# A branch for short expert tiles: gate and up on 32 columns of the array

## The chip, the cores and the metric

The kernel runs on one core of a Trainium2 chip. The metric is the device time of one execution, in microseconds (us). Five engines work beside each other, each with its own stream of instructions: TensorE (PE; its weight loads are PEld), VectorE (DVE), ScalarE (ACT), GpSimd (POOL) and SyncE (SP), which here only starts weight transfers. Each engine branches for itself. A name with a q (PEq, DVEq) is the engine's sequencer.

## The reference, cut to what matters

One decoder layer over 512 tokens of 1024 channels: a mixer (a state-space branch and an attention branch), then a mixture of 16 experts. The change lies in the experts. Each token is sent to two of them:

```
for e in range(16):
    hid = silu(t @ w_gate[e]) * (t @ w_up[e])      # 1024 -> 512, twice
    out = out + gates[:, e:e+1] * (hid @ w_down[e])  # 512 -> 1024
```

with `gates` zero for all but the token's two experts. The kernel computes an expert only for its own tokens, in float32.

## The kernel before, in words

**Stages.** The mixer takes the first 560 us or so, then come routing and, from 577 to 898 us, the experts; a last normalisation ends the kernel. Nothing before or behind the expert stage changes, but for one more small buffer (`sgs`, line 1123) that is cleared early.

**Tiles.** An expert's tokens are cut into tiles of H = 64. A gathered tile `xg` has 128 rows: 64 tokens times two halves of 512 channels. `x_columns` (line 1178) transposes it into `xT`. `body(e, t)` (line 1313) does tile t of expert e in this order on TensorE: `up` (line 1286), then the down product of the tile before (`down`, line 1301; so the silu and the multiplication of this tile have time), `x_columns` of tiles to come, `hidden_columns` (line 1296, transposes of the hidden values) and, for t = 0, the token lists of expert e + 2 (`tile_tokens`, line 1174), which turn ranks into the indices that GpSimd gathers by.

**Gate and up.** `up` runs over 8 parts k of the 1024 channels. For each, the 64 tokens' columns are the stationary operand and 512 columns of the gate weights move through the left half of the array (64 of its columns), 512 of the up weights through the right half. The results stand in one PSUM bank: gate in partitions 0 to 63, up in 64 to 127. `hidden` (line 1292) takes silu of the lower half and multiplies it by the upper.

**Branches.** Tile 0 always runs. Tiles 1 and 2 stand in `tc.If` blocks on the expert's token count (lines 1355 and 1357); tile 2's block lies in that of tile 1. A fourth and later tiles run in ten nested blocks behind the loop (line 1421), which these inputs don't need. What stands in such a block is scheduled as a unit; code outside can be moved ahead of it. That is done today: `up` of the next expert's tile 0 is code outside any block, and a few of its products are issued ahead of line 1355's branch.

**Weights.** An expert has six pieces of 1 MB, loaded by SP into 18 buffers in turn, so three experts ahead; `drop` frees pieces once an expert's products are done, and SP's next transfers start then.

**Order.** `in_order` keeps the written order of TensorE, VectorE and ScalarE instructions within one `with`, not from one `with` to the next.

Of the kernel before, what the change touches and what calls it, by code (L numbers as in the profile page):

```python
# [13 lines left out]
AF = mybir.ActivationFunctionType  # L14
ALU = mybir.AluOpType
AX = mybir.AxisListType

P = 128
# [3 lines left out]
KT = D // P  # L22
# [6 lines left out]
UNIT = 512  # L29
EVAC = 400  # L30
DUE = 8, 4, 4
H = P // 2
INL = 3
MAXO = 10

# [72 lines left out]
def hybrid_layer(ctx: ExitStack, tc: tile.TileContext, A, out):  # L108
    nc = tc.nc
# [127 lines left out]
    class Stream:  # L237
# [7 lines left out]
        def add(self, units, loads, parts):  # L245
            for n, part in enumerate(parts):
                self.parts.append((len(self.raws), n == len(parts) - 1) + part)
            self.raws.append((units, loads))
# [96 lines left out]
    class Experts:  # L345
# [18 lines left out]
        def up(self, e, k):  # L364

            assert self.nload >= 6 * e + 4
            return [self.piece(6 * e + 2 * (k // 4) + n)[:, k % 4 * FF:(k % 4 + 1) * FF] for n in range(2)]

        def down(self, e, k):
            assert self.nload >= 6 * e + 6  # L370
            return [self.piece(6 * e + 4 + k // 2)[:, k % 2 * D + n * 512:k % 2 * D + (n + 1) * 512]
                    for n in range(2)]
# [5 lines left out]
    ew = Experts([(wg_all[e], wu_all[e], wd_all[e]) for e in range(NE)], [])  # L378
# [25 lines left out]
    for j in range(4):  # L404
# [14 lines left out]
        for t, sc_ in enumerate((1, 0)):  # L419
            o = 8 * sc_ + 2 * j  # L420
# [142 lines left out]
    for g in range(4):  # L563
# [17 lines left out]
        for c in range(NT):  # L581
            nc.tensor.matmul(pt[:, c * P:(c + 1) * P], Bc.ap[:, c * P:(c + 1) * P], Cc.ap[:, c * P:(c + 1) * P],
                             start=True, stop=True)
# [14 lines left out]
        for c2 in range(2):  # L598
            pt = tr.get()
            for c in (2 * c2, 2 * c2 + 1):  # L600
                for t in range(2):
                    o = (c % 2) * 256 + t * P
# [19 lines left out]
        for c in (1, 2):  # L622
# [4 lines left out]
                                    op=ALU.add)  # L627
# [71 lines left out]
    for j in range(4):  # L699
# [14 lines left out]
        for hh in range(2):  # L714
            m = FM.alloc(1)
            nc.vector.tensor_tensor(m.v(NT, P), fr[hh].v(NT, P), negm[:, None, :].to_broadcast([P, NT, P]),
                                    op=ALU.subtract)
# [4 lines left out]
        for i in range(NT):  # L722
            w = (i + 1) * P
# [36 lines left out]
        o = FM.alloc(1)  # L760
# [82 lines left out]
    for j in range(8):  # L843
        for y in (ys[j], ya[j]):
            pt = proj(hT, KT)
            t = FM.alloc(1)
# [18 lines left out]
    def rtile(nm, shape, dt=F32):  # L865
        if dt is I32:
            return cp.tile(shape, dt, name=f"rt_{nm}")
        n = 1
        for d in shape[1:]:
            n *= d  # L870
        w = n if dt is F32 else -(-n // 2)
        a = rtc[0][:, rtc[1]:rtc[1] + w]
        if dt is not F32:
            a = a.bitcast(dt)[:, 0:n]
        rtc[1] += -(-w // 2) * 2
        for ax_ in range(len(shape) - 1, 1, -1):
            a = a.rearrange("p (a b) -> p a b", b=shape[ax_]) if ax_ == len(shape) - 1 else \
                a.rearrange("p (a b) c -> p a b c", b=shape[ax_])
        return a
# [8 lines left out]
    half = rtile("half", [P, 1])  # L888
    nc.vector.tensor_scalar(half, pcol, float(H), None, op0=ALU.is_ge)
    nc.vector.tensor_scalar(itb[:, 0:H], itf[:, 0:H], 1.0, None, op0=ALU.add)  # L890
    nc.vector.tensor_copy(itb[:, H:P], itb[:, 0:H])
    itbs = [itb] + [rtile(f"itb{t}", [P, P], BF16) for t in range(1, INL)]
    for t in range(1, INL):
        nc.vector.tensor_scalar(itbs[t], itb, float(t * H), None, op0=ALU.add)
    aux = rtile("aux", [P, NT, NE, 5], BF16)
# [82 lines left out]
    @contextmanager  # L978
    def in_order(engines):

        traced = nc.cur_bb.bb.instructions
        n, prev = len(traced), {}
        yield
        for ins in traced[n:]:
            if ins.engine in engines:
                if ins.engine in prev:
                    tc.add_manual_dep(ins, prev[ins.engine], mybir.DependencyInfo(
                        mybir.DependencyClass.NoSync, mybir.DependencyReason.DATA), reason="in_order")
                prev[ins.engine] = ins.name
# [60 lines left out]
    ET = mybir.EngineType  # L1050
# [63 lines left out]
    xgs, xTs, sgs, yos, ohs = {}, {}, [], [], []  # L1114
# [4 lines left out]
    def clear_early(BM):  # L1119

        for et in kinds:
            xgs[et] = BM.alloc(1).ap
        sgs.extend(BM.alloc(1).ap for _ in range(2))
        for a in (*xgs.values(), *sgs):
            nc.gpsimd.memset(a, 0.0)

    def setup_experts():
# [6 lines left out]
        yos.extend(FM.alloc(1).ap for _ in range(2))  # L1134
        hidT.append(FM.alloc(1).v(4, H))
        for _ in range(3):
# [34 lines left out]
    def tile_ranks(e, t):  # L1171
        onehots(oh_of(e, t), rk[:, :, e], itbs[t])

    def tile_tokens(e, t, n0=0, n1=5):
        tokens(oh_of(e, t), lambda c: aux[:, c, e, :], ixs[e % 3][t], gws[e % 3][t], xgs[e % 2, t], n0, n1,
               128 + 8 * (e % 2 * 3 + t))

    def x_columns(xg, xT):

        pt = tr.get()  # L1180
        for b in range(4):
            nc.tensor.transpose(pt[:, b * P:(b + 1) * P], xg[:, b * P:(b + 1) * P], ident)  # L1182
        nc.scalar.copy(xT, pt)  # L1183
# [21 lines left out]

    NB = S // H - INL
    cnt = rtile("cnt", [P, 16])
# [21 lines left out]
    with in_order((ET.PE, ET.DVE, ET.Activation)):  # L1229
# [15 lines left out]
        BM = Mem(cp, "bm", 48, F32, tags=[f"both{n}" for n in range(12)])  # L1245
        BM.packed = True
        clear_early(BM)
        while BM.room(4):
            ew.raws.append(BM.alloc(4).ap)
# [36 lines left out]
    def up(strm, e, xT, bank):  # L1286
        for k in range(KT):
            for n, w in enumerate(strm.up(e, k)):
                nc.tensor.matmul(bank[n * H:(n + 1) * H], xT[:, (2 * (k % 4) + k // 4) * H:(2 * (k % 4) + k // 4 + 1) * H],  # L1289
                                 w, start=(k == 0), stop=(k == KT - 1))  # L1290

    def hidden(bank, sg):
        nc.scalar.activation(sg[H:P], bank[0:H], AF.Silu)  # L1293
        nc.vector.tensor_tensor(sg[H:P], sg[H:P], bank[H:P], op=ALU.mult)  # L1294

    def hidden_columns(sg):
        for t in range(4):
            nc.tensor.transpose(bhid[:, t * P:(t + 1) * P], sg[:, t * P:(t + 1) * P], ident)
        nc.vector.tensor_copy(hidT[0], bhid.rearrange("p (k s) -> p k s", s=P)[:, :, H:P])
# [13 lines left out]
    def body(e, t):  # L1313

        bank, by, yo, sg = bgu[t], bys[t % 2], yos[t % 2], sgs[t % 2]
        with in_order((ET.PE, ET.DVE, ET.Activation)):
            if t == 0:
                if e + 2 < NE:
                    for u in range(2):
                        tile_ranks(e + 2, u)  # L1320
                tile_ranks(e, 2)
            if t == 1:
                tile_tokens(e, 2)
            up(ew, e, xTs[e % 2, t], bank)
            if e == 0 and t == 0:
                for e_, t_ in early:
                    tile_tokens(e_, t_, 2, 5)
            hidden(bank, sg)
            nc.vector.tensor_copy(ixl[e % 2], ixs[e % 3][t])
            nc.vector.tensor_copy(gwl[e % 2], gws[e % 3][t])  # L1330
            if t:
                down(ew, e, by)
                add(by, yo, ixs[e % 3][t - 1], gws[e % 3][t - 1])
            elif e:
                down(ew, e - 1, by)
                add(by, yo, ixl[1 - e % 2], gwl[1 - e % 2])
                ew.drop(2)
            if t == 0 and e + 1 < NE:
                for u in range(2):
                    x_columns(xgs[1 - e % 2, u], xTs[1 - e % 2, u])  # L1340
            if t == 1:
                x_columns(xgs[e % 2, 2], xTs[e % 2, 2])
            hidden_columns(sg)
            if t == 0 and e + 2 < NE:
                for u in range(2):
                    tile_tokens(e + 2, u)

    n_toks = [nc.values_load(cnti[0:1, e:e + 1], min_val=0, max_val=S) for e in range(NE)]  # L1348
# [49 lines left out]
    def over(t):  # L1398
        if t == 0:
            over_tables()  # L1400
        e_reg = nc.sync.value_load(oei[0:1, t:t + 1], min_val=0, max_val=NE - 1)
        strm = Experts([[w[ds(e_reg, 1)].rearrange("e k n -> (e k) n") for w in (wg_all, wu_all, wd_all)]], spare[0:6])
        strm.load()
        nc.vector.tensor_tensor(rkt, rk[:, :, 0:16], ohe[:, t:t + 1, :].to_broadcast([P, NT, 16]), op=ALU.mult)
        nc.vector.tensor_reduce(rkx, rkt, axis=AX.X, op=ALU.add)
        nc.vector.tensor_scalar(rkx, rkx, ob[:, t:t + 1], None, op0=ALU.subtract)
        for c in range(NT):
            nc.vector.tensor_tensor(auxt[:, c], aux[:, c].rearrange("p e s -> p s e"),
                                    ohe[:, t:t + 1, :].to_broadcast([P, 5, 16]), op=ALU.mult)
        nc.vector.tensor_reduce(auxf, auxt, axis=AX.X, op=ALU.add)  # L1410
        nc.vector.tensor_copy(auxc, auxf)
        onehots(ohs[0], rkx, itb)
        tokens(ohs[0], lambda c: auxc[:, c, :], ixs[0][0], gws[0][0], xgs[0, 0])
        x_columns(xgs[0, 0], xTs[0, 0])
        up(strm, 0, xTs[0, 0], bgu[0])
        hidden(bgu[0], sgs[0])
        hidden_columns(sgs[0])
        down(strm, 0, bys[1])
        add(bys[1], yos[1], ixs[0][0], gws[0][0])
# [40 lines left out]
```

## Time and profile before

| | us |
|---|---|
| median of three runs | 936.26 |
| lowest, highest | 934.28, 937.5 |
| the profiled execution | 936.89 |
| its span, from the first to the last instruction | 935.0 |
| TensorE busy in the span | 846.1 |
| VectorE, ScalarE, GpSimd busy | 535.4, 313.8, 105.2 |

The profile lists, for groups of instructions, the line, the engine, the operation, the operands (out<-in), how many there were, their busy time and mean duration, and how long the engine had been idle before them and what ended that. "Issue" means that nothing the profile shows was waited for. The granted clock (PEclk) is TensorE's share of its full 2.4 GHz.

### The profile page before, as it was taken

The numbers are of one execution on the slowest core, as the hardware profiler recorded it, in microseconds if no ns is written. First come the engines' busy times: TensorE is split into PE (matmuls) and PEld (weight loads), VectorE is DVE, ScalarE is ACT, GpSimd is POOL, SyncE is SP. The second block draws the span as 40 slices with busy tenths as digits, with TensorE's granted clock in tenths as the row PEclk, the third lists the DMA queues.
The fourth block names the chain that finished last, engine by engine and source line by source line (L and its number), as shares of the span: only waits on it lengthen the run. The fifth ranks groups of instructions, "written<-read, shape, count | busy, mean of one in ns | idle before, by whom it ended". The sixth has DMA issues, their size and how long they took to land. (4 is left out here: it accounts for less than half of the span.)

```text
span 935.0 us, 11859 instructions
## 1 busy us (share of the span) xinstructions
PE 846.1 (90%) x4216; PEld 543.5 (58%) x4216; DVE 535.4 (57%) x1310; ACT 313.8 (34%) x561; POOL 105.2 (11%) x117
## 2 busy tenths in 40 slices
PE   2899989999999999999999995999999999999830
PEld 1678778887666677888888892433344333334310
DVE  6849879858876687976745774422342223232123
ACT  5438778444643432522323451101111000011102
POOL 1001000000000000000000021212231222121211
PEclk9899989999999999999999975999999999999985
DMA  9951456313126248895435389698899998549546
GB/s 288 339 146 52 155 164 185 95 41 102 46 68 162 90 150 259 248 294 174 150 101 200 117 326 380 222 367 291 278 389 387 380 356 282 177 141 369 209 113 114
DMA packets 137554, 196.46 MB, mean 210 GB/s; under 512 B 11819, under 2 KB 85723, under 8 KB 137457
## 3 DMA queue, kind: packets, MB, share of 16 engines
q1 hardware_dynamic: 126848, 174.28, 55.0%
q0 software_dynamic: 10160, 20.55, 8.9%
q8 instruction: 46, 0.75, 0.3%
q10 hardware_dynamic: 464, 0.58, 0.2%
q14 instruction: 36, 0.29, 0.1%
HBM read 190.61 MB, written 15.25 MB: 220 GB/s over the span
## 5 line engine op out<-in xcount | busy, mean ns | idle before, releaser
L398 PE MATMUL bank<-rm,rm 128*128 128x512 f32 x512 | 206.4, 407 | 0.4 <-ACT rm L431 0.4
L400 PE MATMUL bank<-rm,rm 128*128 128x512 f32 x512 | 206.5, 403 | 0.0
L399 PE MATMUL bank<-rm,rm 128*128 128x512 f32 x512 | 205.4, 401 | 0.2 <-DVE rm L433 0.2
L1289 PE MATMUL bank<-fm,fm 128*64 128x512 f32 x408 | 125.3, 607 | 3.9 <-issue 1.6
L1289 PE MATMUL bank<-bm,fm 128*64 128x512 f32 x360 | 118.5, 597 | 1.5 <-PEq L1357 0.4
L234 DVE TENSOR_TENSOR rm<-fm,rm 128x1024 fp32r<-128x1024 f32 (+1 forms) x76 | 87.6, 1163 | 42.5 <-ACT rm L233 27.0
L398 PEld LDWEIGHTS bank<-rm,rm 128*128 128x128 f32 x512 | 98.0, 192 | 21.9 <-issue 3.1
L399 PEld LDWEIGHTS bank<-rm,rm 128*128 128x128 f32 x512 | 97.6, 191 | 21.9 <-issue 2.1
L400 PEld LDWEIGHTS bank<-rm,rm 128*128 128x128 f32 x512 | 97.6, 191 | 21.0 <-issue 2.3
L1294 DVE TENSOR_TENSOR bm<-bm,bank 64x512 f32<-64x512 f32 x24 | 16.6, 692 | 151.8 <-ACT bm L1293 143.1
L233 ACT CAST rm<-fm 128x1024 fp32r<-128x1024 f32 (+1 forms) x76 | 75.1, 1007 | 78.3 <-PE bank L399 58.3
L1293 ACT ACTIVATE bm<-bank 64x512 f32<-64x512 f32 x24 | 14.1, 589 | 198.6 <-PE bank L1289 198.6
L1289 PEld LDWEIGHTS bank<-fm,fm 128*64 128x64 f32 x408 | 37.4, 139 | 62.5 <-issue 61.3
L1304 PE MATMUL bank<-bm,fm 128*64 128x512 f32 x256 | 65.6, 593 | 0.7 <-DVEq L1355 0.7
L1289 PEld LDWEIGHTS bank<-bm,fm 128*64 128x64 f32 x360 | 34.7, 136 | 45.6 <-issue 44.4
L390 DVE SCALAR_TENSOR_TENSOR fm<-fm,cact,fm 128x256 f32<-128x256 f32 x112 | 51.2, 480 | 1.8
L1183 ACT COPY fm<-bank 128x512 f32<-128x512 f32 x38 | 20.8, 588 | 85.1 <-PE bank L1182 85.1
L1308 DVE SCALAR_TENSOR_TENSOR fm<-bank,fm,fm 128x512 f32<-128x512 f32 x24 | 18.0, 751 | 47.7 <-PE bank L1304 42.7
L1002 PE MATMUL bank<-rm,rm 128*128 128x512 f32 x192 | 44.2, 391 | 0.3 <-ACT fm L847 0.3
L1162 POOL DMA_INDIRECT bm<-h2d,rt_ix x38 | 39.2, 1032 | 39.0 <-DVE fm L1166 20.4
L1309 POOL DMA_INDIRECT moed<-fm,rt_ixl x16 | 25.7, 1605 | 151.9 <-DVE fm L1308 151.9
L1304 PEld LDWEIGHTS bank<-bm,fm 128*64 128x64 f32 x256 | 21.8, 137 | 36.1 <-issue 34.8
(313 smaller groups left out, 1108.2 us busy)
## 6 DMA issues: line engine op xcount, KB each, us to landing
bm<-in_w_down SPq DMA_DIRECT2D x22, 1024.0 KB
fm<-in_w_in SPq DMA_DIRECT2D x36, 512.0 KB
fm<-in_w_gate SPq DMA_DIRECT2D x17, 1024.0 KB
fm<-in_w_mod SPq DMA_DIRECT2D x16, 1024.0 KB
fm<-in_w_up SPq DMA_DIRECT2D x16, 1024.0 KB
bm<-in_w_up SPq DMA_DIRECT2D x16, 1024.0 KB
bm<-in_w_gate SPq DMA_DIRECT2D x15, 1024.0 KB
fm<-in_w_down SPq DMA_DIRECT2D x10, 1024.0 KB
```

The source lines that it names most:

```text
L233: ins = nc.scalar.copy(hi, src)
L234: nc.vector.tensor_tensor(lo, src, hi.bitcast(F32), op=ALU.subtract)
L390: nc.vector.scalar_tensor_tensor(acc, r, cact[:, k:k + 1], acc, op0=ALU.mult, op1=ALU.add)
L398: nc.tensor.matmul(pt, whi[:, k, :], ah.ap, start=(k == 0), stop=False)
L399: nc.tensor.matmul(pt, whi[:, k, :], al.ap, start=False, stop=False)
L400: nc.tensor.matmul(pt, wlo[:, k, :], ah.ap, start=False, stop=(k == nk - 1))
L1002: nc.tensor.matmul(wps[i][hf], sta.ap[:, tsl], mov.ap[:, hf * 512:(hf + 1) * 512], start=(k == 0 and sta is mh and mov is wh), stop=(k == ...
L1162: nc.gpsimd.indirect_dma_start(out=xg, out_offset=None, in_=h2d2, in_offset=bass.IndirectOffsetOnAxis(ap=ix[:, 0:1], axis=0), bounds_check ...
L1183: nc.scalar.copy(xT, pt)
L1289: nc.tensor.matmul(bank[n * H:(n + 1) * H], xT[:, (2 * (k % 4) + k // 4) * H:(2 * (k % 4) + k // 4 + 1) * H], w, start=(k == 0), stop=(k = ...
L1304: nc.tensor.matmul(bank[n * H:(n + 1) * H], hidT[0][:, k, :], w, start=(k == 0), stop=(k == 3))
L1309: nc.gpsimd.indirect_dma_start(out=moed2, in_=yo, in_offset=None, compute_op=ALU.add, out_offset=bass.IndirectOffsetOnAxis(ap=ix[:, 0:1], ...
```

## The change

`up_few` and `hidden_few` are new. A tile that has at most 32 tokens takes them, all others the old functions. A few-token tile's 32 columns of `xT` are the stationary operand four times: gate and up weights are each cut into two halves of 256 columns, and the four products write PSUM partitions 0, 32, 64 and 96 onward, 256 columns each, so that each uses 32 columns of the array. `hidden_few` takes silu of the two gate quarters into a third buffer and multiplies each by its up quarter into the place where `hidden` leaves the result. The choice is a `tc.If` with an `Else`, inside each of the three tiles' code; the order around it is kept in pieces, before, within each arm, and after.

```
-H = P // 2
+H, Q = P // 2, P // 4
-        sgs.extend(BM.alloc(1).ap for _ in range(2))
+        sgs.extend(BM.alloc(1).ap for _ in range(3))
+    def up_few(strm, e, xT, bank):
+        for k in range(KT):
+            x = xT[:, (2 * (k % 4) + k // 4) * H:(2 * (k % 4) + k // 4) * H + Q]
+            for n, w in enumerate(strm.up(e, k)):
+                for hf in range(2):
+                    o = (2 * n + hf) * Q
+                    nc.tensor.matmul(bank[o:o + Q, 0:256], x, w[:, hf * 256:(hf + 1) * 256], start=(k == 0),
+                                     stop=(k == KT - 1))
+    def hidden_few(bank, sg, tmp):
+        nc.scalar.activation(tmp[H:P, 0:256], bank[0:H, 0:256], AF.Silu)
+        for hf in range(2):
+            o = H + hf * Q
+            nc.vector.tensor_tensor(sg[H:H + Q, hf * 256:(hf + 1) * 256], tmp[o:o + Q, 0:256], bank[o:o + Q, 0:256],
+                                    op=ALU.mult)
@@ body(e, t)
-        with in_order((ET.PE, ET.DVE, ET.Activation)):
+        in_turn = ET.PE, ET.DVE, ET.Activation
+        with in_order(in_turn):
             ...
-            up(ew, e, xTs[e % 2, t], bank)
+        with tc.If(n_toks[e] <= t * H + Q) as few:
+            with in_order(in_turn):
+                up_few(ew, e, xTs[e % 2, t], bank)
+                hidden_few(bank, sg, sgs[2])
+        with few.Else():
+            with in_order(in_turn):
+                up(ew, e, xTs[e % 2, t], bank)
+                hidden(bank, sg)
+        with in_order(in_turn):
             ...
-            hidden(bank, sg)
```

## Rows read from the trace of the kernel before

**Rows 1.** Stretches: us, then each engine's busy time, PEclk, DMA share, GB/s.

```profile
672.00:764.00 92.00, 87.62 (x461) 37.13 (x460) 27.66 (x117) 10.08 (x18) 23.09 (x19) 1.00 1.05 386
764.00:820.00 56.00, 54.75 (x275) 20.13 (x274) 13.29 (x45) 4.60 (x8) 11.11 (x8) 1.00 0.72 238
...
576.00:898.00 322.00, 308.78 (x1590) 122.61 (x1588) 93.83 (x375) 39.09 (x67) 72.14 (x57) 0.99 0.82 291
```

**Rows 2.** Waits, 577 to 900 us: us in total, times, longest.

```profile
POOL moed L1309 <- DVE fm L1308: 225.2, 24, 12.9
```

**Rows 3.** Groups by line and shape, 560 to 910 us: count, busy us, mean ns.

```profile
L1289 PE MATMUL bank<-fm,fm 128*64 128x512 f32 x408 | 125.3, 607 | 3.9 <-issue 1.6 <-PEq L1357 1.3 <-ACT fm L1183 0.3
L1289 PE MATMUL bank<-bm,fm 128*64 128x512 f32 x360 | 118.5, 597 | 1.5 <-PEq L1357 0.4 <-issue 0.4 <-ACT fm L1183 0.3
L1304 PE MATMUL bank<-bm,fm 128*64 128x512 f32 x256 | 65.6, 593 | 0.7 <-DVEq L1355 0.7
...
L1304 PE MATMUL bank<-fm,fm 128*64 128x512 f32 x128 | 32.0, 592 | 0.0
...
L1182 PE MATMUL bank<-ident,bm 128*128 128x128 f32 x152 | 22.4, 289 | 5.1 <-DMA bm<-h2d,rt_ix 5.1
...
L1298 PE MATMUL bank<-ident,bm 128*128 128x128 f32 x96 | 14.6, 275 | 0.1
L1293 ACT ACTIVATE bm<-bank 64x512 f32<-64x512 f32 x24 | 14.1, 589 | 198.6 <-PE bank L1289 198.6
```

**Rows 4.** TensorE in order of time, from 650.1 us: start, us, what.

```profile
650.20 0.59 PE L1289 MATMUL bank<-bm,fm 128*64 128x512 f32 x1
...
650.63 0.59 PE L1289 MATMUL bank<-bm,fm 128*64 128x512 f32 x1
```

**Rows 5.** TensorE in order of time, behind expert 5's tile 0.

```profile
682.35 0.17 PE L1157 MATMUL bank<-fm 128*128 128x5 bf16 x1
682.38 0.24 PE L1159 MATMUL bank<-fm,fm 128*128 128x5 bf16 x4
683.29 0.17 PE L1157 MATMUL bank<-fm 128*128 128x5 bf16 x1 [0.67 <-DVE rt_ix L1161]
```

**Rows 6.** The page: busy us (share) xinstructions; a DMA queue's packets, MB.

```profile
PE 846.1 (90%) x4216; PEld 543.5 (58%) x4216; DVE 535.4 (57%) x1310; ACT 313.8 (34%) x561; POOL 105.2 (11%) x117
...
q8 instruction: 46, 0.75, 0.3%
```

**Rows 7.** Lines 1355, 1421, 1125: duration in ns, min/median/max, first and last start.

```profile
L1355 PEldq COMPARE_BRANCH  x16: 70/316/452, 591.5 to 891.2; - x16
...
L1421 PEldq COMPARE_BRANCH  x1: 3372/3372/3372, 894.6 to 894.6; - x1
...
L1125 POOL MEMSET bm<- x7: 543/544/547, 543.0 to 545.8; 128x512 f32 x7
```

**Rows 8.** TensorE in order of time, behind experts 1 and 14.

```profile
608.42 0.64 PE L1289 MATMUL bank<-bm,fm 128*64 128x512 f32 x1 [0.37 <-issue]
...
883.15 1.94 PE L1289 MATMUL bank<-fm,fm 128*64 128x512 f32 x8 [1.44 <-issue]
```

**Rows 9.** Stretches, for the granted clock (the third number from the end).

```profile
125.30:131.00 5.70, 5.70 (x18) 4.84 (x19) 3.90 (x10) 4.20 (x10) 0.54 (x1) 0.50 0.29 84
...
577.00:581.50 4.50, 4.50 (x14) 1.55 (x14) 1.36 (x8) 2.55 (x5) 0.00 (x0) 0.50 1.05 397
```

**Rows 10.** TensorE in order of time, in the mixer and in expert 0.

```profile
125.30 1.54 PE L603 MATMUL bank<-ident,fm 128*128 128x128 f32 x6 [3.17 <-ACT fm L592]
...
577.63 6.03 PE L1289 MATMUL bank<-fm,fm 128*64 128x512 f32 x17
583.08 0.59 PE L1289 MATMUL bank<-bm,fm 128*64 128x512 f32 x1
```

**Rows 11.** TensorE in order of time, behind expert 2's last tile and expert 4's tile.

```profile
633.12 1.08 PE L1289 MATMUL bank<-fm,fm 128*64 128x512 f32 x4 [0.42 <-PEq L1357]
...
668.97 1.07 PE L1289 MATMUL bank<-bm,fm 128*64 128x512 f32 x2
```

## The prediction

> **What bounds the kernel now.** I read the stretches first. The expert stage, 576 to 898 us, is a third of the span, and TensorE is busy in 308.78 of its 322 us at a granted clock of 0.99; VectorE, ScalarE and GpSimd are busy in 94, 39 and 72 us [rows 1]. The DMA engines, which bring the weights, are full from 672 to 764 us (share 1.05) but not always: 0.72 from 764 to 820, 0.82 over the stage [rows 1]. The waits say the same from the other side: before its scatter-adds GpSimd waited 225.2 us for VectorE's line 1308, the step behind TensorE's down products [rows 2]; its scatters, through which the page's chain of waits runs, are followers. So a microsecond of TensorE in this stage is a microsecond of the kernel, as long as weights keep coming.
>
> Next the groups by line. Line 1289 (gate and up) has 768 matmuls, 408 and 360, for 24 executed tiles (24 silus on line 1293): 32 matmuls and 32 weight loads a tile. Down (line 1304) has 384, or 16 a tile; line 1182 has 152, or 4 for each of 38 gathered tiles, line 1298 4 a tile [rows 3], a token list 5 [rows 5]; each has a weight load beside it. One product of 512 columns is two matmul records, gate and up run side by side on 64 columns each, and pairs start every 0.43 us (650.20, 650.63) [rows 4]: 16 x 0.43 = 6.9 us for one tile's gate and up.
>
> How many tiles take the new branch follows from the reference's routing on its inputs: the experts get 31, 40, 95, 86, 27, 11, 40, 32, 91, 132, 170, 103, 25, 21, 59 and 61 tokens. That makes 24 tiles, as the trace has. At most 32 tokens are in experts 0, 4, 5, 7, 12 and 13 (only tile), 2, 3 and 8 (second tile) and 9 (third): 10 of 24. Ten experts have a single tile and jump over the code of tiles 1 and 2.
>
> **The change part by part**, against the profiled execution's 936.89 us (span 935.0; 0.6 above the median of 936.26).
>
> *Fewer columns at a time: -34.2 us.* A few-token tile issues 8 x 2 x 2 products of 256 columns, 64 matmul records. A column costs 0.43 us / 512, so a record lasts 0.213 us. Four at once: 16 steps, 3.4 us instead of 6.9; ten tiles save 10 x 3.42 = 34.2. No row shows four column groups at once, only two [rows 4]. If only two overlap, nothing is saved; more than 34.2 can't be, since each column group must still take its 16 x 256 columns. I take four: two groups run with no loss at all, each at the full rate. Issue is no limit: four groups need a load and a matmul every 53 ns, and a token list starts its five such pairs within 0.1 us (682.35 to 682.62, less the last one's own 0.17) [rows 5].
> The Trainium skill (TensorE: Matmul & The Clock Gate, Part 3, "Measured speedup vs the span model") measured 2.38x for three 32-column products; by that ratio four would take some 4.3 us a tile, by my estimate, and the sum would be 9 us worse. No run here shows it.
>
> *More code to jump over: +28.5 us.* This decides. The queue that carries instructions moved 46 packets, 0.75 MB, 16 KB each [rows 6]. Counting TensorE's program by the rows above (tile 1: 10 + 64 + 32 + 8 + 8 = 122, tile 2: 104, with branches about 235 for both; each of the ten overflow bodies about 126) gives, with the 8,432 executed records [rows 6] and the code jumped over, some 12,600 instructions, about 270 per packet, an estimate. What a jump costs depends on how far it goes. Line 1355's branches took 70 to 452 ns on TensorE, median 316, and at the longest they skip those 235 instructions, less than a packet. Line 1421's one branch skips ten nested bodies, over 1,200, and took 3372 ns [rows 7]. And twice TensorE runs dry in the middle of gate and up with nothing to wait for, 1.44 us before 883.15 and 0.37 us before 608.42, both put down to "issue" [rows 8]; both come right behind a jump of line 1355 (experts 14 and 1), and by the count both lie where the stream passes two packet limits within a few microseconds. So code beyond the next packet isn't at hand. The change adds 128 instructions and some branches to each of tiles 1 and 2, so line 1355's jump grows from about 235 to about 495, nearly two packets: from almost any place its target lies two packets on. Nine jumps then cost 3.37 instead of 0.32, +27.5; the tenth (expert 15) lies behind down products of expert 14 that hide most of it, +1. The cover is gone by construction: before the jump only token lists of 0.17 us stand in the queue [rows 5]. Bounds: +1 (0.45 each, the dearest of today's jumps) to +34; I take the 3.37 row, because the distance, not the line, is what the two rows differ by.
> The Trainium skill (Runtime: NRT & Kernel Launch, "Instruction fetch mechanics") says that a taken branch to a target outside a window of two pages stalls for a fetch of the page. The trace agrees, with 3372 ns against 316.
>
> *The packet after that is late too: +11 us.* After such a landing the next packet is only then asked for, and gate and up consume 128 instructions in 3.4 us or jump over them. The two dry spells lost 1.44 and 0.37 [rows 8]; I take 1.2 for each of nine. Bounds 0 to 9 x 3.37 = 30.
>
> *The clock: +16 us.* TensorE stood idle for 3.17 us before 125.30 [rows 10], and the stretch from there to 131.0 had a granted clock of 0.50, the lower level of 1.2 GHz [rows 9]. Each long jump idles it for over 3.4 us. On this very stream half clock (577.0 to 581.5, 0.50) made the first 17 records of expert 0 last until 583.08, 5.45 us for what is 8.5 x 0.43 = 3.65: 1.8 us lost [rows 9, 10]. 9 x 1.8 = 16. Bounds 0 to 9 x 2.85 (half of 5.7) = 26.
>
> *24 new branches: +8 us.* Each of five engines branches; only TensorE's counts. A branch that falls through is 70 ns, a jump up to 0.45 [rows 7], and where an arm must level its count first TensorE stood 0.42 us (line 1357) [rows 11]. I take 0.33 x 24. Bounds: 2 (all fall through under queued work) to 21 (0.45 + 0.42 each).
>
> *Cover that goes: +8 us.* Today one to five pairs of the next expert's gate and up run ahead of line 1355's branch, between the token lists (668.97) or after them, beside the branch [rows 11]; inside a branch of its own the product can't. Of 15 experts each loses about 0.43 us, five of them also the 0.67 us that TensorE waits between lists where no pair fills it [rows 5]. 6.5 + 1.5 (part of the five). Bounds 0 to 15 x 1.1 = 16.
>
> *At nothing:* silu on 256 columns instead of 512 (0.59 us) [rows 3] and two multiplies of 32 x 256 lie beside down's 3.4 us, and would cost up to 1 us a tile without it. One more memset on GpSimd (0.54 us) [rows 7], early, beside the last norms. SP's loads of the expert after next issue from places outside the new branches; it only passes one more branch. The third buffer fills the eighth unit of two four-unit tiles, so the weight pieces stay 18.
>
> Sum: -34.2 + 28.5 + 11 + 16 + 8 + 8 = +37.3, 936.9 + 37.3 = 974 us.
>
> **The rivals.**
> *Code is at hand after all: 919 us, faster.* If the jump of 495 costs what one of 235 does, the three terms of 28.5, 11 and 16 go: 936.9 - 34.2 + 8 + 8 = 919. For it: one long row only, and that over four packets, not two. Against: the two dry spells came at one packet's distance. The sign turns where a long jump, with all that follows it, costs 18.2 / 9 = 2 us.
> *Four don't run side by side: 1008 us.* Then 34.2 comes back. For it: no row with four. Against: two lose nothing.
> *Weights become the bound.* They keep the DMA engines busy for 0.82 x 322 = 264 us [rows 1], and the stage without long stalls would still take 304. Only in the full stretch from 672 to 764 us can they be late, and three few-token tiles lie there (experts 5, 7, 8): at most 10 us, and only on top of the first rival, 929.
>
> **How the numbers follow.** Forecast 0.70, between 945 and 1015; code at hand 0.20, 905 to 930, weights included; four not together 0.06; the stall but neither late packets nor clock, 936.9 - 34.2 + 28.5 + 8 = 939, 0.04. Runs of this kernel differ by up to 0.3%, so within 2.8 us is no change. Faster 0.21, same 0.03, slower 0.76. The range, 925 to 1015, leaves out most of the faster case and the sum of all upper bounds.
>
> **What would show it.** Line 1355's ten long branches on TensorE at 3 us and more, TensorE idle after them, stretches at 0.50 behind them in the stage's clock. Line 1289's successor in few-token tiles: 64 records in about 3.4 us. The count of 16 KB packets well above 46. If line 1355 stays under 0.5 us, the forecast is wrong and the time is near 919; if few-token tiles take 6.9 us, it is over 1000.

## The result, and the profile after

| | before | changed |
|---|---|---|
| median, us | 935.28 | 1076.14 |
| lowest, highest | 934.28, 937.5 | 1073.14, 1077.06 |
| span of the profiled execution | 935.0 | 1073.6 |
| ratio, 95% interval | | 1.1483 [1.1456, 1.151] |

The change makes the kernel slower by 140.9 us. The forecast had the sign, 974 us, and missed the size: the time lies 61 us above the upper end of its range.

The expert stage first: the row that answers to the last of [rows 1], and two shorter stretches in it. Columns as there.

```profile
576.00:1036.00 460.00, 310.06 (x1910) 125.18 (x1910) 94.40 (x386) 37.42 (x67) 71.94 (x57) 0.82 0.59 204
597.00:611.00 14.00, 6.28 (x21) 2.18 (x22) 1.42 (x8) 0.00 (x0) 1.99 (x2) 0.51 0.65 234
...
713.00:730.00 17.00, 5.48 (x16) 1.60 (x17) 3.29 (x19) 0.00 (x0) 2.04 (x2) 0.51 0.77 269
```

The stage is 138 us longer. TensorE is busy for 310.06 us instead of 308.78, so it is idle for 149.9 us instead of 13.2: nearly the whole loss is idle time. The busy time should have fallen by the 34.2 us of the forecast; it didn't, because the granted clock of the stage fell from 0.99 to 0.82, with whole stretches at 0.51, which is the lower level of 1.2 GHz. That took the forecast gain back: 310.1 - (308.8 - 34.2) = 35.5 us.

The groups by line, which answer to [rows 3] (lines 1289, 1304, 1298 and 1182 of before are 1289, 1321, 1315 and 1182 here; 1299 is the new product):

```profile
L1321 PE MATMUL bank<-bm,fm 128*64 128x512 f32 x256 | 77.7, 717 | 28.9 <-PEq L1380 14.2 <-issue 11.5 <-DVEq L1380 1.3
L1289 PE MATMUL bank<-fm,fm 128*64 128x512 f32 x240 | 77.4, 638 | 2.8 <-issue 2.8
L1289 PE MATMUL bank<-bm,fm 128*64 128x512 f32 x208 | 74.5, 680 | 11.1 <-issue 10.6 <-ACT fm L1183 0.3
...
L1299 PE MATMUL bank<-fm,fm 128*32 128x256 f32 x336 | 30.3, 431 | 0.4 <-ACT fm L1183 0.3
L1299 PE MATMUL bank<-bm,fm 128*32 128x256 f32 x304 | 26.7, 399 | 0.0
...
L1182 PE MATMUL bank<-ident,bm 128*128 128x128 f32 x152 | 24.9, 304 | 27.0 <-DMA bm<-h2d,rt_ix 27.0
L1315 PE MATMUL bank<-ident,bm 128*128 128x128 f32 x96 | 15.2, 281 | 19.3 <-DVE bm L1311 10.4 <-DVE bm L1306 8.9
```

Line 1299 has 640 records, 64 for each of ten tiles; line 1289 has 448, 32 for each of 14. So the branch goes where the token counts said. The idle time before lines 1182 and 1315 is new: 27.0 us for gathered rows (5.1 before) and 19.3 us for the hidden values (0.1 before).

One short tile, expert 7, in order of time on TensorE:

```profile
772.87 1.09 PE L1182 MATMUL bank<-ident,bm 128*128 128x128 f32 x8
773.89 3.66 PE L1299 MATMUL bank<-bm,fm 128*32 128x256 f32 x64
779.07 0.66 PE L1315 MATMUL bank<-ident,bm 128*128 128x128 f32 x4 [1.52 <-DVE bm L1306]
...
783.21 0.17 PE L1157 MATMUL bank<-fm 128*128 128x5 bf16 x1 [3.37 <-DVE fm L1166]
```

The 64 records take 3.66 us. But look at what follows. Behind gate and up should come down, then x_columns, then hidden_columns (line 1315). Here x_columns stands *before* gate and up, down too, and hidden_columns comes right behind, with 1.52 us of waiting for the multiplication that down used to cover. Then the second token list waits 3.37 us for VectorE. Both are waits of the order, not of the branch. In the waits of the stage (engine, line, waited for: us, times, longest):

```profile
PE bank L1157 <- DVE fm L1166: 47.8, 16, 7.9
DVE rt_ixl L1354 <- DMA moed<-fm,rt_ixl: 47.3, 10, 7.8
...
PE bank L1182 <- DMA bm<-h2d,rt_ix: 27.0, 12, 5.3
...
PE bank L1321 <- PEq L1380: 17.6, 5, 5.7
...
PE bank L1321 <- issue: 16.3, 9, 3.1
...
PE bank L1289 <- issue: 13.4, 6, 7.0
...
PE bank L1315 <- DVE bm L1311: 10.4, 7, 1.5
...
PE bank L1315 <- DVE bm L1306: 8.9, 5, 2.8
```

The second row names the wait that I had not seen coming. Line 1354 copies the last token list of an expert into one of two buffers, from which the scatter-add reads its indices. It waits for a DMA, the scatter of the expert two before, and everything on VectorE behind it waits too. Expert 1 shows the whole chain; VectorE, then TensorE:

```profile
618.46 0.75 DVE L1325 SCALAR_TENSOR_TENSOR fm<-bank,fm,fm 128x512 f32<-128x512 f32 x1 [0.47 <-PE bank L1321]
626.53 0.15 DVE L1354 COPY rt_ixl<-rt_ix 128x1 int32<-128x1 int32 x1 [7.32 <-DMA moed<-fm,rt_ixl]
...
626.66 0.41 DVE L1316 COPY fm<-bank 128x256 f32<-128x256 f32 x1
626.99 0.27 DVE L1161 TENSOR_SCALAR rt_ix<-bank,fm 128x1 int32<-128x1 f32 x1
627.18 0.15 DVE L1166 TENSOR_REDUCE fm<-bank 128x1 f32<-128x3 f32 x1
```

```profile
619.72 0.17 PE L1157 MATMUL bank<-fm 128*128 128x5 bf16 x1
...
627.39 0.17 PE L1157 MATMUL bank<-fm 128*128 128x5 bf16 x1 [7.40 <-DVE fm L1166]
...
631.08 1.09 PE L1289 MATMUL bank<-bm,fm 128*64 128x512 f32 x1 [3.42 <-issue]
```

Line 1325 is the add step of expert 0, whose scatter starts at its end. The copy that follows belongs to expert 2, one branch ahead: it needs the buffer which that scatter still reads, and stands 7.32 us. Behind it stand expert 1's hidden copy and token list, and so TensorE's next list (7.40 us). Only then does the sequencer reach line 1380, the jump over tiles 1 and 2 (line 1355 before), and TensorE idles 3.42 us more. The jump itself takes 0.43 us this time; the larger part is the next branch, line 1342, where expert 2's tile jumps over the new arm:

```profile
L1380 PEldq COMPARE_BRANCH  x1: 426/426/426, 627.4 to 627.4; - x1
```

```profile
L1342 PEldq COMPARE_BRANCH  x1: 2464/2464/2464, 628.4 to 628.4; - x1
```

All sixteen passes of line 1380 on TensorE (count; ns shortest, median, longest), and the queue that brings code, against the 46 packets of [rows 6]:

```profile
L1380 PEldq COMPARE_BRANCH  x16: 73/430/5677, 597.7 to 1026.4; - x16
```

```profile
q8 instruction: 70, 1.15, 0.4%
```

Before, no jump of line 1355 took over 452 ns [rows 7].

### The profile page after: what moved, and what is told of

Same layout as the page of the kernel before. It is cut to its first block, busy times and chain, and to the rows that moved or that the text cites. A ratio compares the mean times of both kernels' runs of the same rounds, so it can differ in the third digit from the quotient of the medians.

```text
span 1073.6 us, 12636 instructions
## 1 busy us (share of the span) xinstructions
PE 845.3 (79%) x4536; PEld 544.8 (51%) x4536; DVE 535.6 (50%) x1320; ACT 311.9 (29%) x561; POOL 105.4 (10%) x118
## 5 line engine op out<-in xcount | busy, mean ns | idle before, releaser
L1321 PE MATMUL bank<-bm,fm 128*64 128x512 f32 x256 | 77.7, 717 | 28.9 <-PEq L1380 14.2
L1289 PE MATMUL bank<-bm,fm 128*64 128x512 f32 x208 | 74.5, 680 | 11.1 <-issue 10.6
L1289 PE MATMUL bank<-fm,fm 128*64 128x512 f32 x240 | 77.4, 638 | 2.8 <-issue 2.8
L1311 DVE TENSOR_TENSOR bm<-bm,bank 64x512 f32<-64x512 f32 x14 | 9.7, 692 | 132.0 <-ACT bm L1310 113.5
L1321 PEld LDWEIGHTS bank<-bm,fm 128*64 128x64 f32 x256 | 21.6, 162 | 74.1 <-issue 68.4
L1310 ACT ACTIVATE bm<-bank 64x512 f32<-64x512 f32 x14 | 8.2, 588 | 150.5 <-PE bank L1289 150.5
L1157 PE MATMUL bank<-fm 128*128 128x5 bf16 (+2 forms) x42 | 7.1, 169 | 50.7 <-DVE fm L1166 47.8
L1182 PE MATMUL bank<-ident,bm 128*128 128x128 f32 x152 | 24.9, 304 | 27.0 <-DMA bm<-h2d,rt_ix 27.0
L1289 PEld LDWEIGHTS bank<-bm,fm 128*64 128x64 f32 x208 | 22.1, 156 | 44.3 <-issue 43.7
```

Of the source, the lines that this page charges most:

```text
L1321: nc.tensor.matmul(bank[n * H:(n + 1) * H], hidT[0][:, k, :], w, start=(k == 0), stop=(k == 3))
```

## The experiments

Theory A: cutting the order into pieces let instructions cross the branch, and that is most of the loss. Theory B: the longer jump and code that comes late are. Lines and names in the diffs are those of the changed kernel; a ratio is to the kernel before on the same chip, with its 95% interval.

**1. The order tied again.** First instructions of each piece are queued behind the last ones of the piece before, on the three engines.

```
+ahead  = last instruction per engine of the first piece
-with in_order(in_turn):            # each arm
+with in_order(in_turn, ahead):
+behind = last instruction per engine of the arm
-with in_order(in_turn):            # third piece
+with in_order(in_turn, behind):
```

> The changed kernel with its three pieces tied into one order again: the branch stays behind what is written before it, and what is written behind it stays behind it, on TensorE, VectorE and ScalarE. Theory A (order): the cut chain let the list copies of the next tile cross the branch on VectorE, where they waited 47.3 us for scatters, and let down and x_columns cross it on TensorE, so that hidden_columns waits 1.5 us uncovered in a dozen tiles. By A the time falls by 47 + 19 and by what the clock gives back, to 970 to 1005, and the waits on line 1354 are gone. Theory B (jumps alone): the longer jumps over tiles 1 and 2 and the code that comes late make the time; by B it stays above 1045.

986.16 us, 1.0548 [1.0513, 1.0583]. This lies in theory A's range: the order is worth 1076.14 - 986.16 = 90 us, more than the whole of my forecast's balance. Its stage:

```profile
576.00:947.00 371.00, 284.53 (x1910) 125.07 (x1910) 94.44 (x385) 37.06 (x67) 72.10 (x57) 0.87 0.73 253
```

TensorE's idle time falls from 149.9 to 86.5 us. Of what is left, 68.5 us are put down to the jump over tiles 1 and 2 or to "issue" before gate, up and down.

**2. Four list buffers.** The changed kernel, untied; the copy still crosses the branch but finds a free buffer.

```
-ixl, gwl = two buffers each, index e % 2
+ixl, gwl = four buffers each, index e % 4
```

> The changed kernel with four buffers instead of two for the last list of an expert (ixl, gwl), nothing else: a copy that has crossed the branch no longer finds its buffer in use by a scatter. Theory A (order): the 47.3 us that VectorE waited on line 1354 go, with the token lists behind them and some of the clock: 1005 to 1035, with down still ahead of the branch. Theory B (jumps alone): TensorE would have waited for its code anyway; above 1060.

1046.05 us, 1.1183 [1.1153, 1.1212]: 30 us better, outside both ranges, and less than theory A's. The wait before line 1354 is gone; TensorE's for gathered rows is not:

```profile
PE bank L1321 <- PEq L1380: 27.3, 7, 6.2
PE bank L1182 <- DMA bm<-h2d,rt_ix: 25.3, 11, 5.2
```

Part of the wait only changes its name. TensorE waits 8.7 us for lists on line 1157 instead of 47.8, but 27.3 us for the jump instead of 17.6, and 18.9 us instead of 13.4 for "issue" before line 1289.

**3. Tied, and the branch in tile 0 alone.**

```
-with tc.If(n_toks[e] <= t * H + Q) as few:   # every tile
+if t == 0: the same with tc.If(n_toks[e] <= Q)
+else: up, hidden, without a branch
```

> Tied as in the first run, and the branch in tile 0 only, so that the jump over tiles 1 and 2 is as long as in the kernel before (about 235 instructions). Six of the ten short tiles keep the gain, 6 x 3.43 = 20.6 us. By A and B alike the long jump is gone: 936 - 20.6 + 8 of lost cover (no gate and up pair can run between the token lists any more) = 923, 912 to 935. If the branch itself is dear (a third theory, C), 945 or more.

970.47 us, 1.0364 [1.033, 1.0398]. The forecast of this run, 923, missed by 47 us, the most telling of the misses. By its range alone it could be theory C, a dear branch; experiment 8 decides against that. The jump over tiles 1 and 2 is short again (428 ns at the longest), but what lies behind it is late: before four tiles of more than 32 tokens (experts 2, 6, 8 and 14) the jump over the new arm takes 5.1 to 5.4 us, and three short tiles run dry in the middle of the arm. Expert 7 on TensorE:

```profile
718.06 1.06 PE L1305 MATMUL bank<-bm,fm 128*32 128x256 f32 x15 [0.92 <-PEq L1397]
722.94 1.50 PE L1305 MATMUL bank<-bm,fm 128*32 128x256 f32 x12 [3.82 <-issue]
```

The records before the gap run at full pace, then 3.82 us of nothing, then the same product goes on. By my count some 235 instructions are skipped and some 30 consumed (15 matmul records and their weight loads) within two microseconds, and the packet behind them isn't there: in the trace the next packet of code begins at 720.49, lasts 1.07 us, and TensorE goes on 1.4 us after its end.

**4. The old kernel with a longer jump.** Code that never runs is added to tiles 1 and 2; nothing else changes.

```
 body(e, 1)
+with tc.If(n_toks[e] > S - 1): up twice (128 instructions, never run)
...
 body(e, 2)
+with tc.If(n_toks[e] > S - 1): up twice
```

> The kernel before with 128 TensorE instructions more at the end of tile 1's and of tile 2's code, behind a condition that never holds, so that the jump over both tiles is about 495 instructions, as in the changed kernel, and nothing else changes. By my prediction's terms for the jump, the late packet and the clock: 936 + 28 + 11 + 16 = 991, 965 to 1010. If the length of the jump costs nothing: within 3 us of 936. If it costs only where nothing covers it: 940 to 960.

998.82 us, 1.0679 [1.0652, 1.0705]: the length of the jump costs 63.5 us, less 0.9 us that TensorE waits for the eight added branches that are passed. All ten long jumps (line 1368 here) took 3.4 to 6.6 us. Stretches of the first, the second, the sixth and the last but one of them; the last three columns are the granted clock, the DMA engines' share and GB/s:

```profile
590.80:594.20 3.40, 0.87 (x4) 0.00 (x0) 1.37 (x8) 0.00 (x0) 1.47 (x2) 1.00 0.27 82
608.40:614.30 5.90, 1.90 (x10) 0.44 (x8) 1.52 (x8) 0.00 (x0) 2.05 (x2) 1.00 0.95 341
...
742.70:749.30 6.60, 0.68 (x2) 0.00 (x0) 1.14 (x7) 0.00 (x0) 2.04 (x2) 0.65 0.92 308
...
936.20:939.90 3.70, 0.73 (x2) 0.00 (x0) 0.19 (x1) 0.02 (x1) 1.16 (x1) 0.91 0.22 28
```

```profile
L1368 PEldq COMPARE_BRANCH  x16: 70/4214/6586, 590.8 to 951.9; - x16
```

A jump takes some 3.5 us where the DMA engines are a quarter busy (0.22 and 0.27) and some 6 or more where they are three quarters busy or full (seven jumps, 0.73 to 1.05); the last takes 4.8 beside 0.35. The trace has the packets of the code queue too, and they tell which part grows. Each of the ten jumps ends 1.3 to 1.5 us after the end of a 16 KB packet, and that packet lasts 0.9 to 1.3 us under either load. But it begins 1.0 us after the start of the jump in the two jumps beside 0.22 and 0.27, and 3.5 to 4.2 us after it in the seven. So the code isn't moved more slowly, it starts later. That it waits behind the weights fits the shares and isn't shown by itself.

What TensorE waited for at these jumps (us, times, longest), 45.3 us in all:

```profile
PE bank L1295 <- PEq L1368: 42.4, 9, 6.0
...
PE bank L1310 <- PEq L1368: 2.9, 1, 2.9
```

**5. VectorE and ScalarE tied, TensorE loose.**

```
-tie the pieces on PE, DVE, ACT
+tie the pieces on DVE, ACT
```

> As the tied kernel (986.2), but only VectorE's and ScalarE's pieces are tied; TensorE's are loose as in the changed kernel, so down and x_columns stand ahead of the branch again, and the list copies do not. Theory A1: the order's 90 us (1076.1 - 986.2) are some 30 for the lists, as four list buffers gave, and some 60 for TensorE's order; by A1 1035 to 1050. Theory A2: nearly all of it is VectorE's order, list copies and token lists together, and TensorE's order costs little; by A2 985 to 1010.

1015.07 us, 1.0864 [1.0828, 1.0899], between the two theories. VectorE's and ScalarE's order is worth 1076.1 - 1015.1 = 61 us; the list copies gave 30 in experiment 2, where TensorE then waited longer for the jump. With that tied, TensorE's order is worth 1015.1 - 986.2 = 29. With VectorE tied the 27.0 us of waits for gathered rows are gone, which points to the token lists that VectorE did late. hidden_columns (line 1323 here) still waits where down doesn't cover it:

```profile
PE bank L1323 <- DVE bm L1319: 10.4, 7, 1.5
...
PE bank L1323 <- DVE bm L1314: 4.6, 3, 1.5
```

**6. Tied, the new arm never taken.**

```
-with tc.If(n_toks[e] <= t * H + Q) as few:
+with tc.If(n_toks[e] > S - 1) as few:        # never holds here
```

> The tied kernel with a condition that never holds in place of the token count: the same code, the same jumps over tiles 1 and 2, but all 24 tiles take the old gate and up, behind a jump over the new arm. Theory D (the gain comes through): 986.2 + 10 x 3.43 = 1020, 1012 to 1030. Theory E (the code eats it): in the six single-tile experts TensorE waits for code that is counted from the jump on, and a product that ends sooner only waits longer; then only the four short second and third tiles gain: 986.2 + 4 x 3.43 = 1000, 993 to 1008.

1004.65 us, 1.0729 [1.0707, 1.0751]. The new arm gives 1004.65 - 986.16 = 18.5 us, not 34.3; by the total it is theory E. In the stage

```profile
576.00:968.00 392.00, 313.03 (x1586) 126.80 (x1586) 92.72 (x376) 38.74 (x67) 72.14 (x57) 0.90 0.70 239
```

TensorE is idle for 79.0 us; with the new arm taken (experiment 1) it is busy 28.5 us less and idle 7.5 us more, at 0.87 instead of 0.90.

But the gain isn't lost where theory E says. I measured from the start of one jump over tiles 1 and 2 to the start of the next, in both traces. With the new arm, experts 7, 12 and 13 are 3.4 to 4.3 us shorter, and expert 0, from its first product on, 3.5 us: all four have a single tile, and each gains at least the whole 3.4, where theory E has nothing. Only expert 5 behaves as theory E wants: it is 1.7 us longer, since TensorE waits for code either way, at the branch here (first row) and at the jump before it in experiment 1 (second row). Experts 6, 8 and 15, which take the old arm in both, are 1.2 to 1.6 us longer. So theory E's total came out by luck.

```profile
L1351 PEldq COMPARE_BRANCH  x1: 5169/5169/5169, 687.8 to 687.8; - x1
```

```profile
L1390 PEldq COMPARE_BRANCH  x1: 6221/6221/6221, 675.4 to 675.4; - x1
```

**7. The old kernel with a jump of 305.** As experiment 4, with 64 instructions in tile 2 alone.

```
 body(e, 2)
+with tc.If(n_toks[e] > S - 1): up once
```

> The kernel before with 64 TensorE instructions more at the end of tile 2's code alone, never executed: the jump over tiles 1 and 2 is about 305 instructions instead of 235 (kernel before) or 495 (941 to 998.8). Theory P (packets): a jump is free as long as its target lies in the packet at hand or the next, and costs a whole fetch otherwise, so each of the ten jumps takes under 0.5 or over 3.3 us and nothing between, and some two to four of the ten are long: 945 to 965. Theory L (length): every jump costs in proportion, 0.3 + 6 x 70/260 = 1.9 us each: about 952, with no jump over 3 us. Theory N: under 300 or so nothing: 935.

954.64 us as a median of four that spread from 942.87 to 960.71, so no ratio is given and the time decides nothing. (No earlier run took the 941 us that the expectation names.) The jumps speak for theory P: in the profiled run (949.72) two of the ten long jumps took 6.08 and 6.02 us, seven 0.32 to 0.42, and only one, of 1.26 us, lies between. Behind the first of the two:

```profile
681.47 1.07 PE L1295 MATMUL bank<-fm,fm 128*64 128x512 f32 x2
688.05 1.98 PE L1295 MATMUL bank<-fm,fm 128*64 128x512 f32 x4 [5.51 <-PEq L1368]
```

But for that one, a jump is almost free or costs a whole fetch. Why the four runs differ isn't shown, since only one was profiled.

**8. Down ahead of the branch.** Experiment 3, with 3.4 us of products between the jump and the branch, and token lists ahead of hidden_columns.

```
 tile_ranks(e, 2)
+if e: down(ew, e - 1, by); add; ew.drop(2)
 with tc.If(n_toks[e] <= Q) as few:
...
-elif e: down(ew, e - 1, by); add; ew.drop(2)
-hidden_columns(sg); tile_tokens(e + 2, 0 and 1)
+tile_tokens(e + 2, 0 and 1); hidden_columns(sg)
```

> The kernel with the branch in tile 0 only (970.5), with the down product of the expert before written ahead of the branch instead of behind it, and the token lists ahead of hidden_columns instead of behind: so 3.4 us of products stand between the jump over tiles 1 and 2 and the branch, and the list waits lie beside silu. Theory B (code that comes late behind the jump made the 5 us stalls of that kernel): eight experts lose 3.4 us less, the lists 0.7 to 1.1 us less in each: 970 - 27 - 10 = 933, 928 to 945. If the stalls only move (the fetch starts later as well): 958 to 970.

938.56 us, 1.0027 [1.0009, 1.0045], 32 us better than experiment 3 with the same branches: theory B. The edit moves the token lists too, so the 32 us belong to both moves together. TensorE's waits for "issue" before gate and up, 28.5 us before the old product and 10.9 before the new one in experiment 3, are gone; most that are left are for VectorE, 20.8 us of them for token lists (12.4 in experiment 3).

**9 to 12. Towards a faster kernel.** Four variants of experiment 8. 9: one token list on each side of hidden_columns, list copies behind its copy.

```
-tile_tokens(e + 2, 0 and 1); hidden_columns(sg)
+tile_tokens(e + 2, 0); hidden_columns(sg); copies to ixl, gwl; tile_tokens(e + 2, 1)
```

> The kernel with the branch in tile 0 only and down ahead of it (938.6), with one token list ahead of hidden_columns and one behind, and the two list copies on VectorE behind its copy of the hidden columns. In the 938.6 TensorE waits 1.1 us for the second list and 1.0 us for that copy in each of ten single-tile experts, and 1.1 + 0.6 in the others. If the waits go and nothing takes their place: 938.6 - 10 x 1.6 - 5 x 1.2 = 917, 912 to 928, faster than the kernel before. If code that comes late is what is left (theory B): the time given back is lost at the branch again, 930 to 940.

937.24 us, 1.0013 [0.9997, 1.0028]: no gain over the kernel before, and far from the 917. 10: the arms of 9 swapped.

```
-If n_toks[e] <= Q: up_few  Else: up
+If n_toks[e] > Q: up  Else: up_few
```

> As the woven kernel, with the arms swapped: the old product first, the new one as the other arm, so that a long tile falls into its 64 instructions and a short one jumps over 64 instead of a long one jumping over 128. By theory B the four single-tile experts of more than 32 tokens lose no stall at the branch (4.3 and 2.1 us at two of them in the 938.6 kernel): 3 to 8 us under the woven one. If the arms' order doesn't matter: within 3 us of it.

937.69 us, 1.003 [1.0011, 1.0049]: 0.5 us from experiment 9, so the order of the arms makes no difference that shows. 11: the order of 9 without branch and new arm.

```
-If n_toks[e] <= Q: up_few, hidden_few  Else: up, hidden
+up(ew, e, xTs[e % 2, t], bank); hidden(bank, sg)
```

> The woven order without any branch and without the new arm: all tiles take the old product. It says what the order alone is worth. If the woven order is about as good as the kernel before's: 930 to 940, and the new arm in tile 0 is worth up to 6 x 3.43 = 20 us against it. If the gain of the woven kernels is the order's own: within 3 us of them.

950.55 us, 1.0158 [1.0138, 1.0179]. So the woven order by itself is 14 us worse than the old one, and the branch with the new arm in six tiles gives 13.3 of at most 20.6 us against it. 12: 9 with VectorE's steps in stricter order.

```
-first piece of an expert free to move ahead of the expert before's end
+tied behind it; copies to ixl, gwl behind tile_tokens(e + 2, 1)
```

> The woven kernel (937.2), with the first piece of each expert tied behind the expert before it and the two list copies behind the second token list. In the woven kernel three rank steps of the next expert (0.57 us) and two list copies (0.2 us) stand on VectorE between the first list and the copy that down waits for, and TensorE then idles 0.9 to 1.3 us, and runs at half clock for 7 us behind three such places. If those steps are what TensorE waits for: 15 x 0.7 = 10 us and some clock, 918 to 929, and faster than the kernel before. If code that comes late takes the place of the wait: 932 to 938.

933.8 us against 938.03 for the kernel before on the same chip, 0.9961 [0.9946, 0.9977]: 0.2 to 0.5% faster than the kernel before. That is not the 918 to 929 I had hoped for; it lies in the other condition's 932 to 938. The kernel before took 936.38 us on this chip in the round of experiment 9, so the gain of 4 us stands beside the 1.7 us by which two rounds there differ. The stage of the profiled run (937.0 us), and what TensorE still waits for:

```profile
576.00:900.00 324.00, 283.85 (x1782) 118.11 (x1782) 92.78 (x382) 37.90 (x67) 72.51 (x58) 0.97 0.81 289
```

```profile
PE bank L1327 <- DVEq L1405: 7.0, 8, 1.0
...
PE bank L1163 <- DVE rt_ixl L1393: 4.0, 6, 0.7
PE bank L1327 <- issue: 3.2, 2, 1.9
...
PE bank L1305 <- DMA fm<-in_w_gate: 2.0, 1, 2.0
```

TensorE is busy for 283.85 us instead of 308.78 [rows 1] and the stage isn't shorter: it idles 40 us instead of 13, in many waits, most of about a microsecond: for VectorE's branch, for token lists, for code, and now for weights. That last row is the rival in which weights become the bound, on a small scale.

## Why the prediction was wrong, and where it was right

Put together from the medians, each step one run against the next: 935.3, + 63.5 for the length of the jump (4), + 5.8 for branches, the jump over the unused arm and lost cover (6 against 4), - 18.5 for the new arm (1 against 6), + 28.9 for TensorE's order (5 against 1), + 61.0 for VectorE's and ScalarE's (the changed kernel against 5): 1076.1. Each term is good to some 3 to 5 us, by the intervals of its two runs. Against the forecast of 974, which started from 936.9, this is 90 us for the order, which had no term, 16 us of the gain that didn't arrive, 8 more for the jump and 10 less for branches and cover. The terms that I had could not have reached it: all five costs at their upper bounds (34, 30, 26, 21 and 16, or 127 us) and no gain at all make 1064.

*The step that failed is "Cover that goes", at +8 us.* It asked only what can no longer move ahead of the branch. The line that decided, that the written order holds within one `with` and not from one to the next, stands in the description of the kernel, and I applied it to the old branch alone. The change cuts one `with` into three, and the code behind a block is free to move ahead of it when its operands allow: down and x_columns did on TensorE, in part at expert 4 and wholly from expert 5 on, and the list copies on VectorE. Cost: 90 us, where the term had no place for any. Experiment 1 shows it by putting the whole order back, experiment 5 by putting back VectorE's and ScalarE's alone, experiment 2 by taking away one wait. The same step undid an item "At nothing": silu and the multiplications were to lie beside down, but down had run ahead, and TensorE stood 19.3 us in 12 waits before hidden_columns.

*The jump: right in kind, and near in sum by errors that cancel.* I had 28.5 + 11 + 16 = 55.5 for the jump, the late packet and the clock; experiment 4 has 63.5. A single jump was mis-sized: 3.37 from the one long row [rows 7], where the DMA share was 0.57; seven of the ten fall at shares of 0.73 and more and take 5.9 to 6.6. So TensorE waited 45.3 us for jumps, not 28.5, and only 0.7 us for code behind them, not 11. In that run's stage the idle time grew by 45 us (58.1 against 13.2) and the busy time by 19 at a granted clock of 0.92, against 16 for the clock. The sum in "How the numbers follow" for the stall without late packets and clock, 939, leaves out one of the two terms of 8 and should be 947.
The Trainium skill (Runtime: NRT & Kernel Launch, "Instruction fetch mechanics") has a taken branch stall when its target lies outside a window of two pages. The trace agrees in part: by my counts jumps of 235 instructions are nearly free, of 305 sometimes not, of 495 never in experiment 4; but of the ten jumps of 495 in the changed kernel, and of the ten in experiment 1, three each took only 0.43 to 0.47 us, which no run here explains.

*Few columns: right per tile, wrong in the sum.* 3.66 us for 64 records against 7.05 to 7.09 for a long tile at full clock, so 3.4 us a tile, as forecast; the rival "four don't run side by side" is out. But only 18.5 of 34.2 us arrived in the total. I priced the gain, the code wait and the clock as independent, and they aren't: with the new arm taken TensorE was idle 7.5 us more, and the granted clock was 0.87 instead of 0.90. By experiment 6's traces single-tile experts can gain in full; where a code wait moved with the gain is seen at expert 5 only, and the rest isn't resolved.
The Trainium skill (TensorE: Matmul & The Clock Gate, Part 3, "Measured speedup vs the span model") gives 2.38x for three products, by which I had estimated 4.3 us; the trace's 3.66 is better than that.

*Branches and lost cover, as I had meant them: too high.* 8 + 8 forecast, 5.8 measured for the two together (6 against 4).

*What I said would show it* was there in part. In the changed kernel only five jumps of line 1380 are over 3 us, not ten. Why the others are short stays open; the waits for lists don't explain it: behind the 7.40 us wait at 627.39 the jump took 0.43 us, behind one of 7.88 at 719.04 it took 3.76, and in neither wait does a packet of code begin. The packets rose from 46 to 70; the 0.50 stretches are there, and longer than one jump explains. "Code at hand", the rival on the faster side, is out by experiment 4; experiment 8 comes close to it with a short jump and 3.4 us of products between two jumps.

What stays open: of VectorE's and ScalarE's 61 us, 30 are the list copies by experiment 2, and the rest I put down to token lists done late, by the waits for gathered rows that left with it; no run took those alone.

## What to carry to other kernels

A branch put into the middle of an ordered sequence can cost more by what it sets free than by itself, here 90 us against some 70: write down for every engine what stands behind the new block and could move ahead of it, and tie it. Count the instructions that a jump skips and those consumed right after it: here jumps over 235 took under half a microsecond, and those that waited for a fetch 3.4 us or, under weight traffic, some 6. Down moved in between the jump and the next branch, with the token lists, bought back 32 us.

## What the runs showed of the hardware that I had not expected

The same jump took 3.40 us beside a DMA share of 0.27 and 6.59 beside 0.92, and the difference lies before the code's packet begins, not in the packet (experiment 4). Two short jumps in a row can be as dear as one long one: 0.3 to 0.4 us for the first, 5.1 to 5.4 for the second, in four of six places (experiment 3). And the kernel of experiment 7 scattered by 18 us over four runs, where the kernel before stayed within 5 in 23.
